# Keys and queries rounded on all rows and placed by transfers, tails in source order, the last joint by token tiles

## The chip, the cores and the metric

The kernel runs on one core of one Trainium2 chip. The metric is the device time of one execution in microseconds (us). PE is the tensor engine, DVE the vector engine, ACT the scalar engine, POOL GpSimd; SP is the engine that issues most DMA transfers, in the order of its program.

## The reference

Two layers of a diffusion backbone work on 256 latent and 256 context tokens of width 1024. Each layer is a half-step SwiGLU, a mixer (retention and differential attention side by side) and a second half-step SwiGLU, each between two RMS norms with shift, scale and gate from a conditioning vector. In the second layer only the latent tokens go on behind the mixer's keys and values.

```python
def modulate(x, g, shift, scale):
    return rmsnorm(x, g) * (1.0 + scale) + shift

def add_residual(x, y, g_post, gate, weight):
    return x + weight * gate * rmsnorm(y, g_post)

def swiglu(h, w_in, w_out):
    a, b = jnp.split(h @ w_in, 2, axis=-1)
    return (jax.nn.silu(a) * b) @ w_out

def diff_attend(q, k, v, lam):
    s = jnp.einsum('bhiqd,bhikd->bhiqk', q, k).astype(jnp.float32) * (DIFF_DH ** -0.5)
    p = jax.nn.softmax(s, axis=-1)
    a = p[:, :, 0] - lam * p[:, :, 1]
    return jnp.einsum('bhqk,bhke->bhqe', a.astype(v.dtype), v)
...
for l in range(DEPTH):
    x = add_residual(x, swiglu(modulate(x, ...)), nw[1], mod[:, 2], 0.5)
    y, yc = token_mixer(h, hc, ...)          # 8 heads of diff_attend, two maps of 64 each; 4 heads of retention
    x = add_residual(x, y, nw[3], mod[:, 5], 1.0)
    x = add_residual(x, swiglu(modulate(x, ...)), nw[5], mod[:, 8], 0.5)
```

Queries and keys of the latent tokens are rotated (rope_2d) before the scores.

## The kernel before, in words

The tokens are four tiles of 128 rows, X0 and X1 latent (LAT), X2 and X3 context (CTX). Every product is three matmuls (`mm3`, L330 to L332): a number is held as a rounded high part and a low part, and high x high, high x low and low x high are summed in PSUM. Weights come as slabs of 128 x 1024 through four raw buffers (`load`, SP's queue) and are split by ACT (L154) and DVE (L155) into one of five buffers; 24 matmuls of 512 columns use a slab. The order in which each engine runs its instructions is fixed before the program starts, by a list scheduler with costs of its own; where the code says `tc.manual_schedule` an engine keeps the order of the source.

A **tail** ends a feed-forward or a mixer: four tiles of 24 matmuls each (two halves of 12), then per tile `post_norm` (Square L317, product L319, residual L325) and, for the next stage, the norm of the two latent tiles: Square L267, mean and power on POOL (L254 to L257), `xn` L270 on DVE, 16 transposes on PE (L280), scale and shift on ACT (L289), high and low parts on DVE (L292, L293). The **last joint** is the place in layer 1 where the mixer ends and the last feed-forward begins; only two tiles are left there.

A mixer has four **blocks** of differential attention (0 to 3), two heads each. `projT` makes the block's transposed keys for all tokens (48 matmuls), then its queries; its result lies in a pair of PSUM banks (main4) until `ev_diff` has taken it out: rotation by quarters (L547, four L550, L552), then high and low parts in 64-row pieces (ACT L571, L575, L577, L578; DVE L572, L576). Each map's tile holds its own 64 rows beside a copy that meets the query's low part, so that a score is two matmuls, L660 with the keys' high and L661 with their low parts. For each head and token tile (a tile of the attention): two maps of scores in a PSUM pair of four banks (side4), row maximum (DVE L662), two exponentials (ACT L665), the difference of the maps (DVE L669, L671, L673), four transposes (PE L682), a copy (ACT L684), four matmuls with the values (L694), and behind the last tile a norm (L699 to L713). Layer 0 has eight such tiles a block, layer 1 four. Between these steps the scheduler puts projections of the next parts on PE.

Of the kernel before, what the change touches and what calls it, by code (L numbers as in the profile page):

```python
# [18 lines left out]
P = 128  # L19
D = 1024  # L20
# [14 lines left out]
def build(ctx, tc, a):  # L35
# [216 lines left out]
    def rstd_2(ss):  # L252
        m = small(2, "pm")
        pool.tensor_scalar(out=m[:, 0:1], in0=ss[:, 0:1], scalar1=1.0 / D, scalar2=EPS, op0=ALU.mult, op1=ALU.add)  # L254
        pool.tensor_scalar(out=m[:, 1:2], in0=ss[:, 1:2], scalar1=1.0 / D, scalar2=m[:, 0:1], op0=ALU.mult, op1=ALU.add)
        r = small(1, "pr")
        pool.tensor_tensor(out=r, in0=m[:, 1:2], in1=cneg[:, 0:1], op=ALU.pow)  # L257
        return r

    def norm_xn(c, alloc):  # L260
        xs = []
        for j in range(2):
            t = 2 * c + j
            ss = small(2, "ss")
            for hf in range(2):
                junk = jp.tile([P, 512], BF16, tag="ja", name="ja")
                act(junk, X[t][:, hf * 512:(hf + 1) * 512], AF.Square, accum_out=ss[:, hf:hf + 1])  # L267
            r = rstd_2(ss)
            xn = alloc([P, D])
            dve.tensor_scalar(out=xn, in0=X[t], scalar1=r, scalar2=None, op0=ALU.mult)  # L270
            xs.append(xn)
        return xs
# [33 lines left out]
    def start(AB):  # L306
        h = new_h()
        norm_pair(LAT, AB, h)
        return h, None

    def post_norm(t, yb, Gb, out=None):
        c = t // 2
        ss = small(2, "ss")
        us = []
        for hf in range(2):
            junk = jp.tile([P, 512], BF16, tag="ja", name="ja")
            act(junk, yb[hf], AF.Square, accum_out=ss[:, hf:hf + 1])  # L317
            u = tmp2()
            dve.tensor_tensor(out=u, in0=yb[hf], in1=Gb[c][:, hf * 512:(hf + 1) * 512], op=ALU.mult)  # L319
            us.append(u)  # L320
            banks.put(yb[hf])
        r = rstd_2(ss)
        for hf in range(2):
            xs = X[t][:, hf * 512:(hf + 1) * 512]
            dve.scalar_tensor_tensor(out=xs, in0=us[hf], scalar=r, in1=xs, op0=ALU.mult, op1=ALU.add)  # L325
            if out is not None:
                nc.sync.dma_start(out[t][:, hf * 512:(hf + 1) * 512], xs)

    def mm3(o, wH, wL, xH, xL, start, stop):
        mm(o, lhsT=wH, rhs=xH, start=start, stop=False)  # L330
        mm(o, lhsT=wH, rhs=xL, start=False, stop=False)  # L331
        mm(o, lhsT=wL, rhs=xH, start=False, stop=stop)  # L332

# [19 lines left out]
    def ffn(l, i, st, AB, fetch, pairs, side, nside, after=None, out=None):  # L353
# [17 lines left out]
        if begun is not None:  # L371
            f0 = len(begun)
            for f in range(f0):
                fin_ev(f, begun[f])
        elif len(pairs) == 2:
            w01 = [fin_w(l, i, 0), fin_w(l, i, 1)]
            ab01 = [[bank(), bank()], [bank(), bank()]]
            fin_mm((0, 1), w01, ab01, 0, 256)
            xs = norm_xn(CTX, tmp4)
            for q in range(4):  # L380
                norm_q(CTX, q, xs, AB, h)
            fin_mm((0, 1), w01, ab01, 256, 512)
            for f in range(2):
                fin_ev(f, ab01[f])
            f0 = 2
# [10 lines left out]
        for f in range(f0, NF):  # L396
            w = fin_w(l, i, f, pin=len(pairs) == 1 and f < 2)
# [39 lines left out]
        tail = [fout_w(NP - 2), fout_w(NP - 1)]  # L437
# [3 lines left out]
        for t in range(NT):  # L441
            for hf in range(2):
                for e in range(2):
                    for j in range(2):
                        fout_mm(t, j, tail[e][0], tail[e][1], False, e == 1 and j == 1, (hf,))
            post_norm(t, y[t], Gb, out)
            if t == 1 and after is not None:
                after()
        slots.put(*tail[0][1], *tail[1][1], *Gb.values())

    def mixer(l, st, AB, fetch, after):
# [69 lines left out]
        def projT(b, pairs, ev, w):  # L521
# [18 lines left out]
            for c in pairs:  # L540
                ev(c, bk[:, :, c * 256:(c + 1) * 256])
# [22 lines left out]
        def ev_diff(H, Lo):  # L564
            def ev(c, b):
                q = rotate(b, dtab, 32) if c == LAT else b
                sl = slice(c * 256, (c + 1) * 256)
                for m in range(2):
                    own, oth = slice(64 * m, 64 * m + 64), slice(64 - 64 * m, 128 - 64 * m)
                    if Lo is None:  # L570
                        act(H[m][own, :, sl], q[own], AF.Copy, scale=0.125)  # L571
                        dve.scalar_tensor_tensor(out=H[m][oth, :, sl], in0=q[own], scalar=0.125,  # L572
                                                 in1=H[m][own, :, sl], op0=ALU.mult, op1=ALU.subtract)
                    else:
                        nc.scalar.copy(H[m][own, :, sl], q[own])  # L575
                        dve.tensor_tensor(out=Lo[m][own, :, sl], in0=q[own], in1=H[m][own, :, sl], op=ALU.subtract)  # L576
                        nc.scalar.copy(H[m][oth, :, sl], q[own])  # L577
                        nc.scalar.copy(Lo[m][oth, :, sl], Lo[m][own, :, sl])  # L578
            return ev
# [291 lines left out]
        def diff_blocks(u, before=None):  # L871
            KH = [slot([P, 2, 512], F32R) for _ in range(2)]
            KL = [slot([P, 2, 512], F32R) for _ in range(2)]
            projT(8 + u, BOTH, ev_diff(KH, KL), 0.3)
# [3 lines left out]
            projT(4 + u, QP, ev_diff(Q, None), 0.3)  # L878
# [73 lines left out]

        NT = 2 * len(QP)
# [20 lines left out]
        fin_early(l, 1, ((0, 0), (0, 1), (1, 0))[:1 if NQ == 2 else 3])  # L974
        Gb = fetch()
        for t in range(NT):
            for hf in range(2):
                for k in range(2 * n0, 8):
                    wo_mm(t, k, w[k - 2 * n0], False, k == 7, (hf,))
            post_norm(t, yb[t], Gb)  # L980
            if t == 1:
                after()
        slots.put(*M.values(), *Gb.values())

# [102 lines left out]
    AB, st0 = startup()  # L1087
    box = [st0]
    for l in range(L):
# [5 lines left out]
        ffn(l, 0, box.pop(), AB, F0, (LAT, CTX), chain(g0, gs1, g1, gs2), 24,  # L1095
            after=lambda: box.append(start(AB1)))
        mixer(l, box.pop(), AB1, F1, after=lambda: box.append(start(AB2)))
        g2, F2 = ada_gate(l, 2, 0.5)
        if last:
            ffn(l, 1, box.pop(), AB2, F2, (LAT,), g2, 5, out=a["out"])  # L1100
        else:
            gs, AB = ada_shsc(l + 1, 0)
            ffn(l, 1, box.pop(), AB2, F2, (LAT, CTX), chain(g2, gs), 13, after=lambda: box.append(start(AB)))


def rope_tables():
# [10 lines left out]
    dt = np.stack([np.concatenate([c, c, c, c], 1), np.concatenate([-s, s, -s, s], 1)], 0)  # L1117
# [10 lines left out]
def layout(i):  # L1128
# [14 lines left out]
    cols[3072:5120] = cols[3072:5120].reshape(32, 2, 2, 16).transpose(0, 2, 1, 3).reshape(-1)  # L1143
# [27 lines left out]
```

## Time and profile before

| | us |
|---|---|
| median of three runs (lowest, highest) | 2194.53 (2194.24, 2195.38) |
| the profiled execution | 2194.1 |
| its span, first to last instruction | 2192.3 |
| PE busy | 2140.4 |
| DVE busy | 1365.7 |
| ACT busy | 865.8 |
| POOL busy | 129.1 |

The clock granted to PE was 0.996 in the mean. The profiled execution is one of the same speed as the runs, so its durations can be set against them. A duration printed for a matmul holds its latency; what the next one waits for is read from start to start. "Idle before" names the instruction whose end let an engine go on.

### The profile page before, as it was taken

The page shows a single profiled execution, that of the slowest core. Times are in us where ns is not written, and L with a number is a line of the kernel's source. Part 1 is how long each engine was busy: PE and PEld are TensorE (multiplying, and loading weights), DVE is VectorE, ACT ScalarE, POOL GpSimd, SP SyncE. Part 2 cuts the span into 40 slices and gives each one's busy share as a digit, 9 for nine tenths or more (in the row PEclk, how much of TensorE's full clock was granted, in tenths as well). Part 3 has the DMA queues.
Part 4 walks back from the last instruction along what each step waited for, and adds up shares of the span by engine and source line. Part 5 has one row for each costly group of instructions (what it writes and reads, how often), then busy time and mean ns, then how long its engine had stood idle before and what let it go on. Part 6 is the DMA issues. An engine that isn't in the chain of part 4 may idle for free. (4 is left out here: it accounts for less than half of the span.)

```text
span 2192.3 us, 27590 instructions
## 1 busy us (share of the span) xinstructions
PE 2140.4 (98%) x10730; PEld 1790.6 (82%) x10730; DVE 1365.7 (62%) x2108; ACT 865.8 (39%) x1367; POOL 129.1 (6%) x236
## 2 busy tenths in 40 slices
PE   7999999999999999999999999999999999998998
PEld 5888888778788878888888888888878888878997
DVE  4799372678665774596243279825347776787554
ACT  3322332553533553522232242223245544565453
POOL 1000000201010000200000010000010000001000
PEclk9999999999999999999999999999999999999999
DMA  8866342222122234364334247734323323355554
GB/s 332 284 218 217 106 135 96 88 68 85 51 91 98 68 97 148 132 211 155 97 124 139 91 161 224 269 96 134 97 67 109 115 93 108 123 194 174 187 183 134
DMA packets 85060, 306.99 MB, mean 140 GB/s; under 512 B 9968, under 2 KB 10048, under 8 KB 84928
## 3 DMA queue, kind: packets, MB, share of 16 engines
q1 hardware_dynamic: 81936, 296.78, 41.2%
q0 software_dynamic: 2848, 8.43, 1.4%
q8 instruction: 84, 1.38, 0.3%
q14 instruction: 48, 0.39, 0.1%
q10 hardware_dynamic: 144, 0.01, 0.0%
HBM read 304.10 MB, written 1.09 MB: 139 GB/s over the span
## 5 line engine op out<-in xcount | busy, mean ns | idle before, releaser
L155 DVE TENSOR_TENSOR w<-raw,w 128x1024 fp32r<-128x1024 f32 x408 | 497.2, 1222 | 465.6 <-ACT w L154 461.9
L154 ACT CAST w<-raw 128x1024 fp32r<-128x1024 f32 x408 | 427.5, 1053 | 665.4 <-PE ps L332 609.3
L330 PE MATMUL ps<-h,w 128*128 128x512 f32 (+1 forms) x1868 | 664.7, 357 | 4.7 <-ACT w L154 2.6
L331 PE MATMUL ps<-h,w 128*128 128x512 f32 (+1 forms) x1868 | 664.9, 356 | 0.4 <-DVE h L293 0.3
L332 PE MATMUL ps<-h,w 128*128 128x512 f32 (+1 forms) x1868 | 663.6, 356 | 1.2 <-DVE w L155 1.2
L330 PEld LDWEIGHTS ps<-h,w 128*128 128x128 f32 x1868 | 353.4, 190 | 57.2 <-DVE h L292 4.7
L332 PEld LDWEIGHTS ps<-h,w 128*128 128x128 f32 x1868 | 353.8, 190 | 50.6 <-DVE w L155 1.8
L331 PEld LDWEIGHTS ps<-h,w 128*128 128x128 f32 x1868 | 354.1, 190 | 50.2 <-DVE h L293 1.4
L174 DVE CUSTOM_DVE_ANT_0 jd<-r,r 128x1024 bf16<-128x1024 f32 x224 | 273.4, 1221 | 6.8 <-DMA r<-wada_dram 2.0
L330 PE MATMUL ps<-w,h 128*128 128x512 f32 x544 | 216.1, 398 | 15.5 <-ACT r L577 11.9
L331 PE MATMUL ps<-w,h 128*128 128x512 f32 x544 | 214.3, 394 | 0.0
L332 PE MATMUL ps<-w,h 128*128 128x512 f32 x544 | 213.8, 394 | 0.0
L330 PE MATMUL ps<-w,gs 128*128 128x512 f32 x504 | 196.2, 389 | 0.0
L331 PE MATMUL ps<-w,gs 128*128 128x512 f32 x504 | 196.1, 389 | 0.0
L332 PE MATMUL ps<-w,gs 128*128 128x512 f32 x504 | 196.1, 389 | 0.0
L366 ACT ACTIVATE t<-ps 128x512 f32<-128x512 f32 (+1 forms) x88 | 47.9, 545 | 252.0 <-PE ps L332 250.6
L330 PEld LDWEIGHTS ps<-w,h 128*128 128x128 f32 x544 | 102.7, 189 | 38.2 <-ACT r L577 15.2
L367 DVE TENSOR_TENSOR r<-ps,t 128x512 f32<-128x512 f32 (+1 forms) x88 | 54.8, 622 | 105.3 <-PE ps L332 77.7
L331 PEld LDWEIGHTS ps<-w,h 128*128 128x128 f32 x544 | 102.8, 189 | 20.2 <-DVE w L155 1.5
L332 PEld LDWEIGHTS ps<-w,h 128*128 128x128 f32 x544 | 102.5, 188 | 20.4
L330 PEld LDWEIGHTS ps<-w,gs 128*128 128x128 f32 x504 | 94.6, 188 | 19.8
L332 PEld LDWEIGHTS ps<-w,gs 128*128 128x128 f32 x504 | 94.6, 188 | 19.6
(180 smaller groups left out, 2132.8 us busy)
## 6 DMA issues: line engine op xcount, KB each, us to landing
raw<-fin_dram SPq DMA_DIRECT2D x176, 512.0 KB, 4.3
r<-wada_dram SPq DMA_DIRECT2D x144, 512.0 KB, 5.1
raw<-fout_dram SPq DMA_DIRECT2D x88, 512.0 KB, 3.6
raw<-winW_dram SPq DMA_DIRECT2D x80, 512.0 KB, 3.6
raw<-winT_dram SPq DMA_DIRECT2D x48, 512.0 KB, 3.6
raw<-wout_dram SPq DMA_DIRECT2D x16, 512.0 KB, 5.6
r<-scr POOLq DMA_DIRECT2D x10, 512.0 KB, 5.4
r<-cc_dram SPq DMA_DIRECT2D x7, 512.0 KB, 5.2
```

The source lines that it names most:

```text
L154: keep(nc.scalar.copy(w[:, 0, :], src))
L155: keep(dve.tensor_tensor(out=w[:, 1, :], in0=src, in1=w[:, 0, :], op=ALU.subtract))
L174: dve.tensor_tensor_reduce(out=junk, in0=r[j], in1=cs[c], scale=1.0, scalar=0.0, op0=ALU.mult, op1=ALU.add, accum_out=out[:, c, 2 * u + j: ...
L330: mm(o, lhsT=wH, rhs=xH, start=start, stop=False)
L331: mm(o, lhsT=wH, rhs=xL, start=False, stop=False)
L332: mm(o, lhsT=wL, rhs=xH, start=False, stop=stop)
L366: act(sg[:, :N], ab[0][:, :N], AF.Silu)
L367: dve.tensor_tensor(out=g[f // 2][:, f % 2, :N], in0=ab[1][:, :N], in1=sg[:, :N], op=ALU.mult)
```

## The change

Four edits. `norm_x` takes the norm's sum of squares in one Square of 1024 columns instead of two, with one POOL step less. `tail` runs PE in the order of the source: the latent norm's transposes stand between the two halves of the fourth tile. Keys and queries are rotated by halves of 64 rows and split for all 128 rows at once (`ev_full`, context first), and transfers on SP's queue (`move`) place the pieces of 32 rows in the maps' tiles: twelve for the keys and eight for the queries of a block, 160 in all; the weight columns and the rotation table are laid out to suit. `last_joint` replaces the last joint: output projection by token tiles, norm and transposes of each tile as it is done, and the first three pieces of the next feed-forward (`head`) with tokens stationary, tile by tile.

```diff
+    def norm_x(t, alloc):
+        ss = small(1, "sx")
+        junk = jp.tile([P, D], BF16, tag="ja", name="ja")
+        act(junk, X[t], AF.Square, scale=1.0 / 32, accum_out=ss)
+        m = small(1, "pm")
+        pool.tensor_scalar(out=m, in0=ss, scalar1=EPS, scalar2=None, op0=ALU.add)
+        r = small(1, "pr")
+        pool.tensor_tensor(out=r, in0=m, in1=cneg[:, 0:1], op=ALU.pow)
+        xn = alloc([P, D])
+        dve.tensor_scalar(out=xn, in0=X[t], scalar1=r, scalar2=None, op0=ALU.mult)
+        return xn
...
+    def tail(NT, part, finish, AB):
+        xs = []
+        with tc.manual_schedule(engines={nc.tensor.engine}):
+            for t in range(NT):
+                part(t, 0)
+                if t == 3 and AB is not None:
+                    h = new_h()
+                    for q in range(4):
+                        norm_q(LAT, q, xs, AB, h)
+                part(t, 1)
+                finish(t)
+                if t < 2 and AB is not None:
+                    xs.append(norm_x(t, tmp4))
+        return None if AB is None else (h, None)
...
+    def last_joint(l, M, fetch, AB):
...
+        with tc.manual_schedule(engines={nc.tensor.engine}):
             for hf in range(2):
...
+                part(0, range(8), hf)
+            post_norm(0, yb[0], Gb)
+            xs = [norm_x(0, tmp4)]
+            for hf in range(2):
+                part(1, range(4), hf)
...
+            part(1, range(4, 8), 0)
+            norm_tile(0, xs[0], AB, h)
+            part(1, range(4, 8), 1)
+            post_norm(1, yb[1], Gb)
+            xs.append(norm_x(1, tmp4))
+            fb = [bank() for _ in range(3)]
+            head(0)
+            norm_tile(1, xs[1], AB, h)
+            head(1)
...
-            for c in pairs:
+            for c in reversed(pairs):
                 ev(c, bk[:, :, c * 256:(c + 1) * 256])
...
+        def move(dst, md, src, ms, n):
+            for rd, rs in zip(rows_of(md), rows_of(ms)):
+                nc.sync.dma_start(dst[rd, :, 0:n].bitcast(F32), src[rs, :, 0:n].bitcast(F32))
+
+        def ev_full(H, Lo, scale):
             def ev(c, b):
-                q = rotate(b, dtab, 32) if c == LAT else b
+                q = rotate(b, dtab, 64) if c == LAT else b
                 sl = slice(c * 256, (c + 1) * 256)
...
+                act(H[:, :, sl], q, AF.Copy, scale=scale)
+                dve.scalar_tensor_tensor(out=Lo[:, :, sl], in0=q, scalar=scale, in1=H[:, :, sl],
+                                         op0=ALU.mult, op1=ALU.subtract)
             return ev
...
-            projT(8 + u, BOTH, ev_diff(KH, KL), 0.3)
+            projT(8 + u, BOTH, ev_full(KH[0], KL[0], 1.0), 0.5)
+            for K2 in (KH, KL):
+                move(K2[1], 1, K2[0], 1, 512)
+                move(K2[1], 0, K2[0], 1, 512)
+                move(K2[0], 1, K2[0], 0, 512)
             if before:
                 before()
             Q = [slot([P, 2, 512], F32R) for _ in range(2)]
-            projT(4 + u, QP, ev_diff(Q, None), 0.3)
+            qH, qL = tmp4([P, 2, 512], F32R), tmp4([P, 2, 512], F32R)
+            projT(4 + u, QP, ev_full(qH, qL, 0.125), 0.5)
+            for m in range(2):
+                move(Q[m], m, qH, m, 256 * NQ)
+                move(Q[m], 1 - m, qL, m, 256 * NQ)
             return KH, KL, Q
```

In the new code `mm3` is L340 to L342, a score L780 and L781, its row maximum L782, exponential L785, difference L789 to L793, transposes L802, copy L804, weighing L814; the eviction is L668 to L673 (rotation), L696 and L697, a move L690, the norm's `xn` L268, `norm_tile` L359 to L369.

The change also moves instructions that it doesn't name. On PE, in block 2 of layer 0, the attention's first tile has just been scored; before, twelve more matmuls of a projection (L330 to L332, weights from the right, tokens h) stand ahead of these rows:

```order
L330 MATMUL ps<-w,h 128x512
L331 MATMUL ps<-w,h 128x512
L332 MATMUL ps<-w,h 128x512
L660 MATMUL ps<-r_5273,r_5359 128x512
L682 MATMUL ps<-ident,t_5474 128x128 x4
L661 MATMUL ps<-r_5275,r_5359 128x512
L660 MATMUL ps<-r_5274,r_5360 128x512
L661 MATMUL ps<-r_5276,r_5360 128x512
L330 MATMUL ps<-w,h 128x512
L694 MATMUL ps<-r_5051,t_5517 128x128 x2
L694 MATMUL ps<-r_5052,t_5517 128x128 x2
L682 MATMUL ps<-ident,t_5505 128x128 x4
```

The same place on PE now, from the second map's scores of the first two tiles (L780, L781) to the transposes of the second (L802):

```order
L780 MATMUL ps<-r_5253,r_5337 128x512
L781 MATMUL ps<-r_5255,r_5337 128x512
L780 MATMUL ps<-r_5253,r_5337 128x512
L781 MATMUL ps<-r_5255,r_5337 128x512
L780 MATMUL ps<-r_5252,r_5336 128x512
L802 MATMUL ps<-ident,t_5455 128x128 x4
L781 MATMUL ps<-r_5254,r_5336 128x512
L780 MATMUL ps<-r_5253,r_5337 128x512
L781 MATMUL ps<-r_5255,r_5337 128x512
L814 MATMUL ps<-r_5030,t_5498 128x128 x2
L814 MATMUL ps<-r_5031,t_5498 128x128 x2
L802 MATMUL ps<-ident,t_5486 128x128 x4
```

The projection matmuls between the scores and the transposes are gone from here; they now stand ahead of the block's first score, 100 of them behind the query projection instead of 35.

On SP, the queue of the weight slabs, at the same block of the kernel before there are slabs alone (raw; winT for transposed projections, winW for wide ones):

```order
L147 DMA raw<-winW_dram 128x1024 x4
L147 DMA raw<-winT_dram 128x1024 x4
L147 DMA raw<-winW_dram 128x1024 x8
L147 DMA raw<-winT_dram 128x1024 x4
L147 DMA raw<-winW_dram 128x1024 x4
```

And now, with the keys' (r_5252 to r_5255) and the queries' moves (r_5336, r_5337):

```order
L147 DMA raw<-winT_dram 128x1024 x3
L690 DMA r_5253<-r_5252 32x1024 x4
L690 DMA r_5255<-r_5254 32x1024
L690 DMA r_5252<-r_5252 32x1024 x2
L690 DMA r_5255<-r_5254 32x1024 x3
L690 DMA r_5336<-t_5338 32x1024
L690 DMA r_5254<-r_5254 32x1024 x2
L690 DMA r_5336<-t_5338 32x1024
L690 DMA r_5336<-t_5339 32x1024 x2
L690 DMA r_5337<-t_5338 32x1024 x2
L690 DMA r_5337<-t_5339 32x1024 x2
L147 DMA raw<-winT_dram 128x1024
```

Twenty moves stand between two slabs, and the last of the keys' moves comes behind the first of the queries'.

## Rows read from the trace of the kernel before

**Rows 1.** The page, parts 1 and 2: PE, its clock, the transfer rate, 40 slices.

```profile
PE 2140.4 (98%) x10730; PEld 1790.6 (82%) x10730; DVE 1365.7 (62%) x2108; ACT 865.8 (39%) x1367; POOL 129.1 (6%) x236
...
PEclk9999999999999999999999999999999999999999
...
GB/s 332 284 218 217 106 135 96 88 68 85 51 91 98 68 97 148 132 211 155 97 124 139 91 161 224 269 96 134 97 67 109 115 93 108 123 194 174 187 183 134
```

**Rows 2.** The waits of PE: us in total, times, the longest.

```profile
PE ps L280 <- DVE t L270: 12.7, 10, 4.9
PE ps L330 <- ACT r L577: 11.9, 8, 1.7
...
PE ps L330 <- DVE t L550: 3.2, 1, 3.2
```

**Rows 3.** Timeline of PE, layer 0, block 0, behind the query projection.

```profile
448.70 0.50 PE L330 MATMUL ps<-w,h 128*128 128x512 f32 x1 [1.66 <-ACT r L577]
```

**Rows 4.** Timeline of ACT at the same place.

```profile
448.07 0.58 ACT L577 CAST r<-ps 64x512 fp32r<-64x512 f32 x1
```

**Rows 5.** Timeline of PE, layer 1, block 3.

```profile
1922.67 0.47 PE L330 MATMUL ps<-w,h 128*128 128x512 f32 x1 [3.21 <-DVE t L550]
...
1924.09 0.50 PE L330 MATMUL ps<-w,h 128*128 128x512 f32 x1 [0.95 <-ACT r L577]
...
1925.07 0.63 PE L330 MATMUL ps<-w,h 128*128 128x512 f32 x1
...
1929.46 0.39 PE L330 MATMUL ps<-w,h 128*128 128x512 f32 x1
...
1932.18 0.39 PE L660 MATMUL ps<-r,r 128*128 128x512 f32 x1
```

**Rows 6.** Timeline of PE in the first tail and in the third.

```profile
390.80 0.65 PE L280 MATMUL ps<-ident,t 128*128 128x128 f32 x4 [1.29 <-DVE t L270]
...
392.63 1.53 PE L280 MATMUL ps<-ident,t 128*128 128x128 f32 x12 [0.48 <-DVE t L270]
...
1262.36 2.75 PE L280 MATMUL ps<-ident,t 128*128 128x128 f32 x12 [0.48 <-DVE t L270]
```

**Rows 7.** Timeline of PE at the last joint.

```profile
1993.63 1.11 PE L280 MATMUL ps<-ident,t 128*128 128x128 f32 x4 [4.92 <-DVE t L270]
...
1995.47 2.82 PE L280 MATMUL ps<-ident,t 128*128 128x128 f32 x12 [0.72 <-DVE t L270]
```

**Rows 8.** DMA issues: count, KB each, median us to landing.

```profile
raw<-winT_dram SPq DMA_DIRECT2D x48, 512.0 KB, 3.6
...
out_dram<-X SPq DMA_DIRECT2D x4, 256.0 KB, 2.1
```

**Rows 9.** Timeline of DVE: blocks 2 and 3, layers 0 and 1.

```profile
718.63 1.22 DVE L662 TENSOR_REDUCE mx<-ps 128x2 f32<-128x1024 f32 x1
...
721.82 0.75 DVE L673 SCALAR_TENSOR_TENSOR t<-t,r 128x512 f32<-128x512 f32 x1
...
747.94 0.48 DVE L673 SCALAR_TENSOR_TENSOR t<-t,r 128x256 f32<-128x256 f32 x1
...
780.16 2.36 DVE L662 TENSOR_REDUCE mx<-ps 128x2 f32<-128x1024 f32 x2
...
812.98 0.48 DVE L673 SCALAR_TENSOR_TENSOR t<-t,r 128x256 f32<-128x256 f32 x1
...
1889.32 2.36 DVE L662 TENSOR_REDUCE mx<-ps 128x2 f32<-128x1024 f32 x2
...
1903.56 0.75 DVE L673 SCALAR_TENSOR_TENSOR t<-t,r 128x512 f32<-128x512 f32 x1
...
1929.66 1.23 DVE L662 TENSOR_REDUCE mx<-ps 128x2 f32<-128x1024 f32 x1 [0.49 <-PE ps L661]
...
1935.46 0.74 DVE L673 SCALAR_TENSOR_TENSOR t<-t,r 128x512 f32<-128x512 f32 x1
...
1947.82 0.75 DVE L673 SCALAR_TENSOR_TENSOR t<-t,r 128x512 f32<-128x512 f32 x1
```

More of the change, by code (lines that the diff above doesn't have):

```diff
@@ L315, in post_norm @@
         for hf in range(2):
-            junk = jp.tile([P, 512], BF16, tag="ja", name="ja")
-            act(junk, yb[hf], AF.Square, accum_out=ss[:, hf:hf + 1])
+            junk = jp.tile([P, D], BF16, tag="ja", name="ja")
+            act(junk[:, 0:512], yb[hf], AF.Square, scale=1.0 / 32, accum_out=ss[:, hf:hf + 1])
             u = tmp2()
@@ L332, in mm3, with split2, norm_tile @@
         mm(o, lhsT=wL, rhs=xH, start=False, stop=stop)
+    def split2(src):
+        w = [slot([P, 2, 512], F32R) for _ in range(2)]
+        wv = [z.rearrange("p a n -> p (a n)") for z in w]
+        nc.scalar.copy(wv[0], src)
+        dve.tensor_tensor(out=wv[1], in0=src, in1=wv[0], op=ALU.subtract)
+        return wv, w
+    def norm_tile(t, xn, AB, h):
+        A, B = AB
+        ts = slice(t * P, (t + 1) * P)
+        for q2 in range(2):
+            bk = bank()
+            b = bk.rearrange("p (k n) -> p k n", k=4)
+            for kk in range(4):
+                k = 4 * q2 + kk
+                nc.tensor.transpose(b[:, kk], xn[:, k * P:(k + 1) * P], ident)
+            hf = tmp2([P, 4, P])
+            for kk in range(4):
+                k = 4 * q2 + kk
+                act(hf[:, kk, :], b[:, kk], AF.Identity, bias=B[:, t // 2, k:k + 1], scale=A[:, t // 2, k:k + 1])
+            banks.put(bk)
+            for q in (2 * q2, 2 * q2 + 1):
+                hv = hf[:, 2 * (q % 2):2 * (q % 2) + 2]
+                hH = h[q][:, :, 0, ts]
+                dve.tensor_copy(hH, hv)
+                dve.tensor_tensor(out=h[q][:, :, 1, ts], in0=hv, in1=hH, op=ALU.subtract)
     early = {}
@@ L351, in fin_part, with ffn @@
                         h[k // 2][:, k % 2, 1, c0:c1], fresh and k == 0, k == KD - 1)
-    def ffn(l, i, st, AB, fetch, pairs, side, nside, after=None, out=None):
+    def ffn(l, i, st, AB, fetch, pairs, side, nside, nxt=None, out=None):
         h, begun = st
@@ L370, in ffn @@
         f0 = 0
-        if begun is not None:
+        if isinstance(begun, dict):
+            g.update(begun)
+            f0 = 3
+        elif begun is not None:
             f0 = len(begun)
@@ L396, in ffn @@
         for f in range(f0, NF):
-            w = fin_w(l, i, f, pin=len(pairs) == 1 and f < 2)
+            w = fin_w(l, i, f, pin=False)
             ab = [bank(), bank()]
@@ L436, in ffn @@
         cs.clear()
-        tail = [fout_w(NP - 2), fout_w(NP - 1)]
+        last2 = [fout_w(NP - 2), fout_w(NP - 1)]
         if i == 1 and l < L - 1:
@@ L440, in ffn, with part @@
         Gb = fetch()
-        for t in range(NT):
-            for hf in range(2):
[L443 to L451, printed above, removed]
+        def part(t, hf):
+            for e in range(2):
+                for j in range(2):
+                    fout_mm(t, j, last2[e][0], last2[e][1], False, e == 1 and j == 1, (hf,))
@@ L452, in mixer @@
+    def mixer(l, st, AB, fetch, nxt):
         h = st[0]
@@ L562, in ev_ret, with rows_of @@
             return ev
-        def ev_diff(H, Lo):
+        def rows_of(m):
+            return [slice(32 * m + 64 * x, 32 * m + 64 * x + 32) for x in range(2)]
+        def move(dst, md, src, ms, n):
+            for rd, rs in zip(rows_of(md), rows_of(ms)):
+                nc.sync.dma_start(dst[rd, :, 0:n].bitcast(F32), src[rs, :, 0:n].bitcast(F32))
+        def ev_full(H, Lo, scale):
             def ev(c, b):
-                q = rotate(b, dtab, 32) if c == LAT else b
+                q = rotate(b, dtab, 64) if c == LAT else b
                 sl = slice(c * 256, (c + 1) * 256)
[L568 to L578, printed above, removed]
+                act(H[:, :, sl], q, AF.Copy, scale=scale)
+                dve.scalar_tensor_tensor(out=Lo[:, :, sl], in0=q, scalar=scale, in1=H[:, :, sl],
+                                         op0=ALU.mult, op1=ALU.subtract)
             return ev
@@ L951, in mixer @@
         flush()
+        if last:
+            return last_joint(l, M, fetch, nxt)
         NT = 2 * len(QP)
@@ L973, in mixer, with part @@
         w = sum((wo_w(u) for u in range(n0, 4)), [])
-        fin_early(l, 1, ((0, 0), (0, 1), (1, 0))[:1 if NQ == 2 else 3])
+        fin_early(l, 1, ((0, 0),))
         Gb = fetch()
[L976 to L982, printed above, removed]
+        def part(t, hf):
+            for k in range(2 * n0, 8):
+                wo_mm(t, k, w[k - 2 * n0], False, k == 7, (hf,))
+        st = tail(NT, part, lambda t: post_norm(t, yb[t], Gb), nxt)
         slots.put(*M.values(), *Gb.values())
+        return st
     def startup():
@@ L1094, in build @@
         gs2, AB2 = ada_shsc(l, 2)
[L1095 to L1097 removed]
+        st = ffn(l, 0, st, AB, F0, (LAT, CTX), chain(g0, gs1, g1, gs2), 24, AB1)
+        st = mixer(l, st, AB1, F1, AB2)
         g2, F2 = ada_gate(l, 2, 0.5)
         if last:
[L1100 removed]
+            ffn(l, 1, st, AB2, F2, (LAT,), g2, 5, out=a["out"])
         else:
             gs, AB = ada_shsc(l + 1, 0)
[L1103 removed]
+            st = ffn(l, 1, st, AB2, F2, (LAT, CTX), chain(g2, gs), 13, AB)
 def rope_tables():
```

94 lines of the change are left out of this document (70 added, 24 removed).

## The prediction

> **What bounds the kernel now.** I read the page's parts 1 and 2 first: the tensor engine (PE) is busy 2140.4 of 2192.3 us and its clock stands at nine tenths or more in every slice of the page [rows 1]. So the time is the matmul work plus the gaps in it, and a change that leaves the products alone can only move gaps. The second view, the waits of PE, lists them: 12.7 us for the normalised rows that the transposes of L280 want, 11.9 us in eight waits for a cast of the key eviction (L577), 3.2 us for a rotation (L550) [rows 2]. The rest is the program's start and smaller waits, which the change doesn't touch. Third, the timelines at these places. At 448.70 PE has idled 1.66 us for a PSUM pair [rows 3] that the scalar engine (ACT) is still emptying with L577 at 448.07 [rows 4], the last but one of a dozen 64-row casts by which a key projection is evicted. In layer 1 the same place costs more: 3.21 and 0.95 us, and behind them the granted clock falls to the lower of its two levels, 1.2 GHz: eight matmuls at 0.43 us each (1925.07 is one) where twelve take 2.72 us, 0.2267 each, from 1929.46 to 1932.18 [rows 5]. The durations printed are latencies; these start-to-start pitches are what work costs: 0.227 us for 512 columns, half of it for 256 (an estimate), about 0.11 for a transpose (twelve in 1.53 us with the last one's latency [rows 6]).
>
> The profiled execution took 2194.1 us, 1.8 outside the span; the median of the runs shown is 2194.53. I sum against 2194.1. What a measurement of this kernel can tell from no change is about 0.2%, 4.4 us.
>
> **The tails.** Each of four tails stalls twice before L280, 1.29 and 0.48 us [rows 6], because the 16 transposes stand behind 64 of 96 matmuls, 16 of them after the last one of tile 1. The new order puts 36 there. What they must cover follows from the old stall: 16 x 0.227 + 1.29 = 4.9 us for the first transposes, and with 4 transposes, 3 matmuls and the second stall 6.5 us for tile 1; 36 x 0.227 = 8.2 us covers both. Gain 4 x 1.77 = 7.1. The single 1024-wide Square and the POOL step left out shorten a chain that is now hidden: nothing. If the cover failed, the 1.77 would come back a tail. At one tail (1262.36) the twelve transposes took 2.75 instead of 1.53 us, at the low clock after the idle time [rows 6]: 1.2 more. Tails: 8.3.
>
> **The last joint.** It idles 4.92 and 0.72 us, and its transposes run at the low clock (2.82 for twelve instead of 1.53; 1.11 for four instead of 0.65) [rows 7]: 7.4 us in sum. In the new order tile 0 is covered by 36 matmuls (8.2 us against 6.5), and tile 1 by head(0), 72 of 256 columns, 8.2 us. But head(1) wants all of tile 1's rows, and after its eight transposes nothing is left to cover ACT's and DVE's making of them: of these eight scale-and-shift steps and the first high and low parts I take 3 us as exposed (bounds 0, and the old 5.6). Six more transposes are 0.7. Gain 7.4 - 3.7 = 3.7.
>
> **The evictions.** K and Q are now rotated by halves (two L671 in place of four L550) and leave PSUM by one ACT and one DVE step of each token half, some seven steps of 0.6 to 0.7 us on two engines in place of twenty: about 4 to 5 us, the context half first. PE asks for the pair after Q's projection of 48 matmuls, 10.9 us (5.5 in layer 1). Seven of the eight L577 waits go: 11.9 - 0.95 = 10.9 us. The eighth, with the 3.21 us of L550 and the slow clock behind it [rows 5], is K of block 3 in layer 1, whose eviction stands behind block 2's softmax on DVE in both orders; I leave its cost as it is (bounds: it all goes, 5.7 us more gain, or it doubles).
>
> **The moves.** 160 transfers of at most 128 KB, 20 a block on SP's queue. The nearest rows are 2.1 us to landing for 256 KB and 3.6 for a weight slab of 512 KB [rows 8]. Q's eviction (5 us), eight moves of 1 MB in all (3.2 us at the 332 GB/s of the first slice [rows 1], an estimate) and one landing make 10 to 12 us behind Q's last matmul. In the new order 92 to 120 matmuls, 20.8 to 27 us, stand between Q's projection and the block's first score, so the moves are hidden. SP is in order: 20 moves wait for Q's eviction with the next weight slabs behind them, some 8 us late; the slabs loaded ahead (four raw and five split buffers, 24 matmuls or 5.4 us each) are worth more. Cost 0; without that cover, up to 3.6 us for each slab that is late. The Trainium skill, "DMA: Bandwidth & Descriptors", section "Rules for kernel authors", says that two transfers to disjoint partition halves serialize and advises one wide transfer; with its fit of 2.0 us plus bytes at 436 GB/s an estimate is 20 x 2.3 = 46 us a block. That speaks against placing keys in 32-row pieces; no run here shows such a transfer yet.
>
> **Where the attention moved.** This is the loss. Before, the first score of a block stood 35 matmuls behind Q's projection; now 92 to 120. The projections that used to stand between the softmax steps are spent before them. In blocks 0 and 1 of each layer 4.98 us of matmuls still stand between the last score of the first tile and its transposes. A tile's softmax, from the row maximum (718.63) to the end of L673 (721.82 + 0.75), took 3.94 us [rows 9]: covered. In blocks 2 and 3 it is not: there the order leaves 0.68, 1.80, 1.74 and 1.81 us, and PE, in order, must wait. Lower bound, the first tile alone: 3.3 + 2.1 + 2.2 + 2.1 = 9.7 us. Upper bound: the whole chain of the block, from the first row maximum to the end of the last L673, keeps its length, 29.8, 33.3, 15.0 and 18.9 us [rows 9]; the matmul work of the order in that stretch falls from 26.7 to 19.0, 30.0 to 23.9, 13.7 to 9.2 and 17.3 to 11.0. (For the first: 44 projection matmuls instead of 76, 10 wide scores instead of 12, 16 narrow ones, 44 transposes and weighings: 10.0 + 2.3 + 1.8 + 4.8 = 18.9.) Less what the old order lost there anyway (3.1, 3.3, 1.3, 1.6): 7.7 + 6.1 + 4.5 + 6.3 = 24.6 us. I take 18, nearer the top: tiles 3 and 4 can't score before the first two have emptied their PSUM pairs, and in block 2 of layer 0 not one projection matmul stands between the first four tiles. Behind block 3 of layer 1 the gate transposes and the output projection wait too: 1.5 (0 to 4).
>
> **Sum.** -8.3 - 3.7 - 10.9 + 18 + 1.5 = -3.4 us: 2190.7, on the runs' median 2191.
>
> **The rivals.**
> *The dense attention costs only its first tiles.* For it: a key eviction takes ten casts from ACT and four steps from DVE, so the later tiles may find both free. Against it: the PSUM pairs. 9.7 instead of 18: 2182, and with block 3's eviction of layer 1 off the path 2177.
> *The softmax queues behind weight splitting (slower).* In block 3 of layer 1 the first tile took 6.54 us (1929.66 to the end of its L673 at 1936.20) with two L155 and two gate steps ahead of it on DVE. In the old order 6.6 us of matmuls hid that; in the dense blocks no more than 1.8 us do. 6.5 us for the first tile of the four is 20 us, and 2.6 more for each later pair (3 + 3 + 1 + 1) is 21: 41 instead of 18, 2214. It decides from 21.4 us in the four blocks, 5.4 a block: above that the kernel is not faster.
> *The moves come later than their cover.* If the pieces of a block went one behind the other, 20 x 2.1 = 42 us, of which K's twelve start 11 us before Q's end, some 10 to 15 us a block would show, 80 to 120 in all: 2290. Against it: the first slice moves 332 GB/s [rows 1] while 512 KB land in 3.6 us [rows 8], which is over two transfers under way at once. The Trainium skill's rule on serializing would be this case.
> *Nothing comes of the eviction.* Then 10.9 us are not gained and it ends near 2202; only with an eviction of over 10.9 us, which its steps don't add up to.
>
> **How the numbers follow.** Forecast with its neighbours (2185 to 2198) 0.42, first rival 0.22, second 0.27, moves 0.04, no gain 0.05. The range leaves out the moves, the far end of the second rival and the very best case: from all bounds at their best, -8.3 - 7 - 16.6 + 9.7 = -22 (2172), to dense blocks at 24.6 and 4 behind them, with no gain at the joint, +9.4, and a part of the queueing on top: 2208. The forecast's own range is 2185 to 2198. Faster by over 0.2% (below 2190.1): half of the forecast's 0.42 and the first rival, 0.44; slower (above 2198.9): second rival, moves, and no gain, 0.34; the rest 0.22.
>
> **What would show it.** In the waits of PE after the change: no L696 or L697 (the new eviction) with more than a us or two, except in block 3 of layer 1; L280 gone from the four tails; at the last joint one wait of about 3 us at L359 or L340. New lines must appear: L802 waiting for L793, L780 for L785, in blocks 2 and 3 only, 10 to 25 us together. If L780 waits for a DMA, the moves are late. The forecast is wrong if the new waits sum to less than 12 or more than 25 us, or if they stand in blocks 0 and 1 as well.

## The result and the profile after

The changed kernel took 2213.31 us (2212.27 to 2213.59, four executions), the kernel before 2194.39 beside it: ratio 1.0085, 95% interval 1.0068 to 1.0103. (Every ratio here is to the kernel before, measured beside the kernel that is named.) It is slower by 19 us; 2191 was forecast, in a range up to 2208.

The page of the changed kernel, parts 1 and 2, answers to [rows 1]:

```profile
PE 2150.4 (97%) x10736; PEld 1805.5 (82%) x10736; DVE 1317.6 (60%) x2059; ACT 802.0 (36%) x1239; POOL 111.1 (5%) x194
...
PEclk9999999999999999999999999999999999899999
```

DVE and ACT have 48 and 64 us less to do and POOL 18: the work went away as meant. PE has nearly the same matmuls (10736 for 10730), so its gaps have grown. Its waits, us in total, times, the longest:

```profile
PE ps L340 <- DVE t L671: 6.0, 2, 3.0
PE ps L341 <- DVE w L155: 4.3, 3, 2.9
PE ps L981 <- ACT t L804: 3.8, 1, 3.8
PE ps L780 <- ACT t L785: 3.8, 2, 3.0
PE ps L342 <- DVE w L155: 3.4, 2, 2.9
PE ps L814 <- ACT t L804: 3.3, 6, 0.7
```

L280's 12.7 us and the eight waits for the eviction's casts [rows 2] are gone, and no score waits for a transfer. What came instead lies inside the attention blocks: scores waiting for exponentials (L785), weighings for copies (L804), projections for a rotation (L671) or for a weight slab that stands behind softmax steps on DVE (L155).

To sum this up by place I took from the trace the time from each matmul's start to the next one's, less the pitch of the earlier one, which is that time in an undisturbed stretch (0.2266 us for 512 columns, 0.1195 for 256, 0.110 for a transpose or weighing). The rest, the gap, holds idle time and slow-clock matmuls alike. In us, with two of the experiments below (e9 and e12):

| place | before | after | e9 | e12 |
|---|---|---|---|---|
| four tails | 14.7 | 6.2 | 6.2 | 6.2 |
| layer 0, blocks 0 and 1 | 4.8 | 17.8 | 2.8 | 5.8 |
| layer 0, blocks 2 and 3 | 5.6 | 15.7 | 4.3 | 15.5 |
| layer 1, blocks 0 and 1 | 1.5 | 1.9 | 1.9 | 2.5 |
| layer 1, blocks 2 and 3 | 2.7 | 26.1 | 2.2 | 22.4 |
| between the blocks (evictions) | 23.7 | 6.8 | 6.3 | 3.1 |
| last joint and just ahead of it | 9.4 | 4.7 | 4.1 | 4.1 |
| all else (start, end) | 18.8 | 20.9 | 20.9 | 20.7 |
| sum | 81.1 | 100.1 | 48.7 | 80.4 |

Tails, evictions and joint give 30 us; the blocks take 47. The end of block 0 of layer 0, on PE in the changed kernel:

```profile
503.48 0.39 PE L342 MATMUL ps<-h,w 128*128 128x512 f32 x1
504.66 0.41 PE L802 MATMUL ps<-ident,t 128*128 128x128 f32 x2 [0.79 <-DVE es L819]
505.53 0.71 PE L814 MATMUL ps<-r,t 128*128 128x128 f32 x4 [0.46 <-ACT t L804]
...
506.97 0.71 PE L814 MATMUL ps<-r,t 128*128 128x128 f32 x4 [0.52 <-ACT t L804]
510.66 0.80 PE L340 MATMUL ps<-w,h 128*128 128x512 f32 x1 [2.98 <-DVE t L671]
511.25 0.63 PE L341 MATMUL ps<-w,h 128*128 128x512 f32 x1
```

Behind 503.48 no projection is left, and the softmax of the last tiles shows as waits of transposes (L802) and weighings (L814). Then the next projection waits 2.98 us for PSUM, and behind the idle time its matmuls run at the lower clock level (granted 0.50 from 511.25 to 515.50; ten matmuls at 0.427 us). DVE in the same block, its idle time in brackets:

```profile
476.83 2.35 DVE L782 TENSOR_REDUCE mx<-ps 128x2 f32<-128x1024 f32 x2 [6.40 <-PE ps L781]
...
484.74 0.68 DVE L681 SCALAR_TENSOR_TENSOR r<-ps,r 128x512 fp32r<-128x512 f32 x1
...
507.59 0.68 DVE L668 TENSOR_TENSOR t<-ps,rtab 128x512 f32<-128x512 f32 x1
...
509.92 0.69 DVE L671 TENSOR_TENSOR t<-ps,rtab 64x512 f32<-64x512 f32 x1
```

Two things stand in these rows. The first score ran at 469.83, yet the first row maximum comes 7.0 us later: it needs both maps, and the order has the second map's first score at 476.18, 28 matmuls behind the first map's. In the kernel before the two are 1.5 us apart, on PE and on DVE:

```profile
457.01 0.50 PE L660 MATMUL ps<-r,r 128*128 128x512 f32 x1
```

```profile
458.50 2.35 DVE L662 TENSOR_REDUCE mx<-ps 128x2 f32<-128x1024 f32 x2
```

And the retention's keys, whose context half leaves PSUM at 484.74 (L681), wait until 507.59 for the rotation of their latent half (L668), behind the whole attention. PE's wait at 510.66 is for that PSUM: the last step that reads it there (L671) ends at 510.61. In layer 1 the queue is another. DVE and PE, block 2:

```profile
1908.35 2.35 DVE L782 TENSOR_REDUCE mx<-ps 128x2 f32<-128x1024 f32 x2 [1.50 <-PE ps L781]
1910.62 1.21 DVE L155 TENSOR_TENSOR w<-raw,w 128x1024 fp32r<-128x1024 f32 x1
```

```profile
1911.89 0.55 PE L342 MATMUL ps<-h,w 128*128 128x256 f32 x1 [2.89 <-DVE w L155]
```

A weight slab's low part, for which ACT was done at 1907.06, stands behind two row maxima that themselves waited for scores. Later in that block the granted clock falls. Two windows: bounds, length, busy time of PE, PEld (weight loads), DVE, ACT and POOL with their instructions, then PE's granted clock, the DMA share and GB/s:

```profile
1906.00:1929.00 23.00, 17.51 (x105) 15.62 (x104) 16.83 (x25) 13.68 (x27) 0.00 (x0) 0.85 0.49 164
1929.00:1937.00 8.00, 6.00 (x19) 4.65 (x18) 5.95 (x14) 1.10 (x3) 1.02 (x1) 0.57 0.00 0
```

### The profile page after: what moved, and what is told of

It is laid out like the page before. It is cut to its first block, busy times and chain, and to the rows that moved or that the text cites. A ratio compares the mean times of both kernels' runs of the same rounds, so it can differ in the third digit from the quotient of the medians.

```text
span 2211.8 us, 27624 instructions
## 1 busy us (share of the span) xinstructions
PE 2150.4 (97%) x10736; PEld 1805.5 (82%) x10736; DVE 1317.6 (60%) x2059; ACT 802.0 (36%) x1239; POOL 111.1 (5%) x194
## 5 line engine op out<-in xcount | busy, mean ns | idle before, releaser
L155 DVE TENSOR_TENSOR w<-raw,w 128x1024 fp32r<-128x1024 f32 x399 | 486.1, 1221 | 458.1 <-ACT w L154 455.0
L340 PE MATMUL ps<-h,w 128*128 128x512 f32 (+1 forms) x1820 | 653.4, 360 | 6.0 <-ACT w L154 3.0
L342 PE MATMUL ps<-h,w 128*128 128x512 f32 (+1 forms) x1820 | 652.1, 359 | 3.5 <-DVE w L155 3.4
L154 ACT CAST w<-raw 128x1024 fp32r<-128x1024 f32 x399 | 418.9, 1055 | 650.2 <-PE ps L342 578.5
L341 PE MATMUL ps<-h,w 128*128 128x512 f32 (+1 forms) x1820 | 652.0, 359 | 0.4 <-DVE h L293 0.3
L340 PEld LDWEIGHTS ps<-h,w 128*128 128x128 f32 x1820 | 345.2, 190 | 58.5 <-DVE h L292 4.7
L342 PEld LDWEIGHTS ps<-h,w 128*128 128x128 f32 x1820 | 345.4, 190 | 53.1 <-DVE w L155 4.4
L341 PEld LDWEIGHTS ps<-h,w 128*128 128x128 f32 x1820 | 345.6, 190 | 50.3 <-DVE h L293 1.4
L340 PE MATMUL ps<-w,h 128*128 128x512 f32 (+1 forms) x552 | 218.8, 398 | 9.4 <-DVE t L671 6.0
L341 PE MATMUL ps<-w,h 128*128 128x512 f32 (+1 forms) x552 | 218.5, 396 | 4.4 <-DVE w L155 4.3
L342 PE MATMUL ps<-w,h 128*128 128x512 f32 (+1 forms) x552 | 217.3, 394 | 0.0
L340 PE MATMUL ps<-w,gs 128*128 128x512 f32 x504 | 196.2, 389 | 0.0
L342 PE MATMUL ps<-w,gs 128*128 128x512 f32 x504 | 196.1, 389 | 0.0
L340 PEld LDWEIGHTS ps<-w,h 128*128 128x128 f32 x552 | 105.8, 192 | 31.8 <-DVE t L671 6.7
L341 PEld LDWEIGHTS ps<-w,h 128*128 128x128 f32 x552 | 105.6, 191 | 26.9 <-DVE w L155 7.0
L342 PEld LDWEIGHTS ps<-w,h 128*128 128x128 f32 x552 | 105.6, 191 | 21.5 <-DVE h L293 0.4
L342 PEld LDWEIGHTS ps<-w,gs 128*128 128x128 f32 x504 | 94.6, 188 | 19.8
L340 PEld LDWEIGHTS ps<-w,gs 128*128 128x128 f32 x504 | 94.6, 188 | 19.7
```

Of the source, the lines that this page charges most:

```text
L154: keep(nc.scalar.copy(w[:, 0, :], src))
L155: keep(dve.tensor_tensor(out=w[:, 1, :], in0=src, in1=w[:, 0, :], op=ALU.subtract))
```

## The experiments

**Which part loses.** e1 is the change without the placement of K and Q, e2 that placement alone in the kernel before; e7 adds to e1 one line of the placement:

```diff
-            for c in pairs:
+            for c in reversed(pairs):
                 ev(c, bk[:, :, c * 256:(c + 1) * 256])
```

> Everything of the change but the placement of keys and queries: they are evicted in 64-row pieces as before. The comparison of the two traces puts the gain of the four tails at 8.6 us and of the last joint at 7.3, and the loss in the attention blocks. Theory (the loss is the attention moved behind its cover): 2194.4 - 8.6 - 7.3 = 2178, with a range of 2175 to 2182. Rival (tails and joint themselves disturb the mixers that follow them, and the gains seen in the trace are only shifted): 2188 or more.

> The kernel before with only the new eviction and the transfers of keys and queries. Theory: the blocks lose 47 us and the waits for the key eviction give back 14, so 2194.4 + 33 = 2227 (2220 to 2232). Rival (the loss comes from the parts together, for instance from tails that end at another point of the weight stream): near 2200.

> e1_tails_joint (2182.6: all of the change but the placing of K and Q) with one line of the placement kept: K's projection evicts its context half first. It moves no row, and the first scores stand 48 matmuls behind Q's last. Theory (the eviction's waits of the kernel before come from ScalarE's first cast waiting for VectorE's rotation, which a half without rotation spares; 11.9 us of waits): 2171 us (2168 to 2180). Rival (the four casts and six other steps of the old eviction still queue, and the later scores take the rest): 2182 us or more.

Measured: e1 2182.58 (ratio 0.9942, 0.9928 to 0.9957), e2 2217.91 (1.0103, 1.0088 to 1.0118), e7 2173.32 (0.9907, 0.9892 to 0.9922). So the placement is the part that loses, 23 us, and the rest gains 13; together they lose 9 more than their sum. The waits of PE for the eviction, in e1 and in e7:

```profile
PE ps L340 <- ACT r L698: 11.9, 8, 1.7
...
PE ps L340 <- DVE t L671: 3.2, 1, 3.2
```

```profile
PE ps L340 <- DVE t L671: 5.3, 8, 1.0
```

The context half first takes 10 us of these waits away (15.1 to 5.3) without moving a row, and some 8 us of the time (by the ratios).

e8 is the changed kernel with the old last joint: the call of `last_joint` is taken out, and the old code with its own early weight loads stands there again.

> The changed kernel with the old last joint (the old order and loads there, all else of the change kept). If the three parts add up, it gives back what the joint earned, 8.55 - 1.25 = 7.3 us: 2220 us (2217 to 2223). If the joint's early loads and weight splits collide with the softmax of the last attention block, which the placement made late (the whole is 8 us worse than the sum of e1 and e2), the old joint takes nothing or gains: 2205 to 2211 us.

Measured: 2211.71 (1.0082, 1.0067 to 1.0097), against 2213.31: the parts don't add up. The gaps say why: at its place the new joint saves 7.1 us (8.4 to 1.25), but block 3 ahead of it grows from 7.2 to 12.2 and the stretch between them from 0.2 to 3.5. In the changed kernel ACT, and behind it PE, hold this there:

```profile
1975.09 1.04 ACT L347 CAST r<-raw 128x1024 fp32r<-128x1024 f32 x1 [2.30 <-DMA raw<-wout_dram]
1976.04 0.58 ACT L804 COPY t<-ps 128x512 f32<-128x512 f32 x1
```

```profile
1976.68 1.03 PE L981 MATMUL ps<-ident,t 128*128 128x128 f32 x4 [3.76 <-ACT t L804]
```

The joint's slab (L347) came late, the attention's copy stood behind it, and PE waited 3.76 us for that copy. In e1, where block 3 is not late, the joint keeps its gain.

**Transfers, or the later place?** e3 leaves all transfers out (the second map reads the first map's keys, and the queries are evicted straight into the tiles that the scores read). e4 is e3 with the transfers made to tiles that nothing reads. e5, e6 and e11 are e3 with the attention held back (the last number is 5 in e5, 8 in e6, 10 in e11):

```diff
-            if sideq:
+            if sideq and clock[0] >= sideq[0][4]:
...
-            defer(f"d{u}", diff_attn(u, *kq, dv), within, 4 * NQ + LAG + 1)
+            defer(f"d{u}", diff_attn(u, *kq, dv), within, 4 * NQ + LAG + 1, 8)
```

> The changed kernel without its 160 transfers: both maps' scores read the one tile that the eviction wrote, so the attention's numbers are other ones; operations and shapes of PE, DVE and ACT are the same. Its order has the first score 26 matmuls behind the query projection instead of 92 to 120. Theory: the blocks' loss goes and the evictions' gain stays, 2213 - 47 = 2166 (2162 to 2178). Rival (the one-piece eviction or the order of DVE behind it is the cause): 2200 or more.

> As the run without transfers, but 160 transfers of the same sizes on the same queue go to tiles that nothing reads, so that no score waits for them; the attention's numbers are other ones here too. Theory (only the wait and the place of the scores cost): within 4 us of the run without transfers. Rival (traffic, or SP standing still with weight slabs behind it): over 10 us slower than that run.

> The kernel of e3_no_transfers (no transfer at all; both maps read one tile, so the attention's numbers differ) with each attention held back at the moment it is handed to the matmul order: its first score stands 60 matmuls behind Q's last in every block, against 26 there. Theory (the changed kernel loses by the later place of the attention, not by a wait for a transfer): between e3's 2161.5 and e6_hold8, 2175 to 2190 us. Rival (a later place is harmless as long as nothing waits for a transfer): 2160 to 2168 us.

> As e5_hold5, held back further: first score 96 matmuls behind Q's last, where the changed kernel has it in most blocks, and still without a transfer (attention's numbers differ as in e3). Theory (the later place is the loss): near the changed kernel's 2213 less the 5.6 us that idle transfers cost in e4, so 2200 us (2192 to 2210), with the waits for L819's and L804's tiles at the ends of layer 0's blocks back. Rival (the transfers' landing or their traffic is the loss): 2160 to 2170 us.

> As e6_hold8 (no transfers; attention's numbers differ as in e3), held to 144 matmuls behind Q's last in the first three blocks, 33 us, which is past the changed kernel's first row maximum (30 us). Theory (there is a latest place, between 24 and 30 us behind Q for the first row maximum, past which the cover runs out): gaps of 6 us or more at the ends of layer 0's blocks and 2185 to 2215 us. Rival (lateness never matters here; what costs is that the two maps' scores stand apart, or the transfers): 2172 us or less.

Measured:

| kernel | first score behind Q, matmuls | us | ratio (95%) |
|---|---|---|---|
| e3 | 26 | 2161.50 | 0.9849 (0.9834 to 0.9864) |
| e4 | 26 | 2167.11 | 0.9877 (0.9861 to 0.9894) |
| e5 | 60 | 2159.87 | 0.9846 (0.9831 to 0.9860) |
| e6 | 96 | 2166.42 | 0.9876 (0.9859 to 0.9892) |
| e11 | 144 (first three blocks) | 2171.20 | 0.9886 (0.9871 to 0.9900) |

Moves that nothing reads cost 5.6 us, between the theory's 4 and the rival's 10. One place of layer 1 has a gap of 7.1 in e4, where e3 has under 2: PE waits 1.68 and 2.14 us for the two halves of a weight slab, and the slow clock follows. Whether the transfers' bytes make that, or their place in SP's queue and in the order, isn't shown.

My first theory, that a later first score by itself makes the loss, falls: at 96 matmuls e6 takes 47 us less than the changed kernel (5.6 of them for the moves, by e4), and e11, which the theory put at 2185 or more, loses no more than 10 against e3. What differs is in their rows. In e6 both maps' scores stand together, so the first row maximum comes 23.7 us behind Q's last matmul (29.9 in the changed kernel) and the last weighing starts at 497.27, while projections still run between the weighings. On DVE and PE:

```profile
470.19 2.35 DVE L782 TENSOR_REDUCE mx<-ps 128x2 f32<-128x1024 f32 x2
```

```profile
497.27 0.69 PE L814 MATMUL ps<-r,t 128*128 128x128 f32 x4
```

In e11 the attention ends at 511.8, later than in the changed kernel, but its code comes later too, and DVE has the retention's rotation ahead of the first row maximum:

```profile
480.77 0.68 DVE L668 TENSOR_TENSOR t<-ps,rtab 128x512 f32<-128x512 f32 x1
481.46 1.39 DVE L671 TENSOR_TENSOR t<-ps,rtab 64x512 f32<-64x512 f32 x2
482.88 1.23 DVE L782 TENSOR_REDUCE mx<-ps 128x2 f32<-128x1024 f32 x1
```

**The same transfers, another order.** e9 changes one line, and e13 is its control, with all moves on GpSimd's queue:

```diff
-            for rd, rs in zip(rows_of(md), rows_of(ms)):
-                nc.sync.dma_start(dst[rd, :, 0:n].bitcast(F32), src[rs, :, 0:n].bitcast(F32))
+            for i, (rd, rs) in enumerate(zip(rows_of(md), rows_of(ms))):
+                (nc.sync, pool)[i].dma_start(dst[rd, :, 0:n].bitcast(F32), src[rs, :, 0:n].bitcast(F32))
```

> The changed kernel with one line changed: of each pair of 32-row moves the second is issued from GpSimd's queue instead of SyncE's. The same transfers, but in the kernel's written-out order the first map's scores now stand 50 matmuls behind Q's last (96 before) and the second map's 15 behind those (28 before). First theory (a later first score alone is the loss) has fallen with e6_hold8. Theory now: the loss is that the second map's first score stands 124 matmuls behind Q, so that the first row maximum, which needs both maps, comes 30 us behind Q and the chain of softmaxes outlasts the projection that covers it; with 65 matmuls (15 us) the blocks' gaps return to some 2.5 us and the time to 2167 to 2180 us. Rival (attention that truly waits for its transfers loses by the transfers themselves, their landing or their traffic): 2195 us or more, with waits for a DMA at the first scores.

> The changed kernel with all its moves issued from GpSimd's queue instead of SyncE's, a control for e9_two_queues, which changed both the queue and the place of the scores. The first scores stay 99 matmuls behind Q and the second map's 28 behind those. Theory (the place in the order is the loss): 2195 to 2216 us. Rival (what helped in e9 was SyncE's queue, rid of the moves ahead of the weight loads): 2175 us or less.

e9: 2162.37 (0.9851, 0.9836 to 0.9865), 51 us less than the changed kernel, and 11 less than e7. The first scores of its two maps and the row maximum in block 0:

```profile
457.93 0.39 PE L780 MATMUL ps<-r,r 128*128 128x512 f32 x1
...
461.33 0.39 PE L780 MATMUL ps<-r,r 128*128 128x512 f32 x1
```

```profile
461.98 2.35 DVE L782 TENSOR_REDUCE mx<-ps 128x2 f32<-128x1024 f32 x2 [2.99 <-PE ps L781]
```

The row maximum comes 15.6 us behind Q's last matmul (446.37) and no score waits for a transfer. Yet a move of the keys takes longer to land than in the changed kernel (second fence):

```profile
r<-r SPq DMA_DIRECT2D x48, 128.0 KB, 4.0
r<-r POOLq DMA_DIRECT2D x48, 128.0 KB, 4.0
```

```profile
r<-r SPq DMA_DIRECT2D x96, 128.0 KB, 2.3
```

A block's last move lands only 1.7 us earlier behind Q (12.6 for 14.2 us in block 0). What changed more is the order fixed before the run: it puts the scores 50 and 65 matmuls behind Q instead of 100 and 128. e13: 2204.69 (1.0051, 1.0034 to 1.0068), with the scores at 99 and 127: the other queue brings 9 us, though one score now waits 1.1 us for a move; the other 42 come with the order. In e13 the gaps of layer 0's first two blocks are 6 to 7 us, block 0's chain from the first row maximum to the last weighing being 3.3 us shorter, and those of layer 1's last two some 30, as bad as ever.

e10 keeps SyncE's moves and lets PE run the blocks as the code writes them, the attention held to 60 matmuls (`tc.manual_schedule` around the blocks).

> The changed kernel, its transfers untouched, with TensorE's order through the four blocks as the code writes it, and the attention held to 60 matmuls (13.6 us) behind Q's last, both maps' scores together. Theory (the order is the loss, the transfers are not): the transfers land 14.7 us behind Q, so about 1 us of wait a block, and 2167 to 2185 us; the written order may add waits of its own, since it does not look at how long a softmax takes. Rival (the transfers are the loss): 2200 us or more.

2293.49 (1.0440, 1.0422 to 1.0457): the worst of all, and past the 2200 that was written for the rival. Its waits don't bear the rival out, but the run is no test of the theory either, since the written order brings waits of its own everywhere:

```profile
PE ps L340 <- DVE t L900: 27.1, 20, 5.2
...
PE ps L780 <- DMA r<-t: 5.1, 3, 1.8
```

The second line is of use: with the scores 60 matmuls behind Q, three do wait for a query move, 1.8 us at most. That bounds the true place of the transfers.

**The tie behind the attention.** e12 is the changed kernel with the rotation's scratch from another ring:

```diff
-            q, w = tmp2([P, 2, 256]), tmp2([P, 2, 256])
+            z = slot([P, 2, 512])
+            q, w = (z[:, i].rearrange("p (j n) -> p j n", j=2) for i in range(2))
+            slots.put(z)
```

> The changed kernel, with the two scratch tiles of a rotation taken from the ring of 20 slots instead of the ring of five t2 tiles, which the attention's transposed weights share. Transfers, queues and the places of the first scores stay (100 and 128 matmuls behind Q); but the rotation of the retention's K now stands on VectorE behind the third row maximum instead of behind the whole attention, so that PSUM comes free earlier and 111 matmuls of projection stand inside block 0 instead of 92. Theory (the late attention costs because the next projection's rotation, and with it the PSUM that the matmuls behind it need, is tied behind it): the gaps of layer 0's first two blocks fall from 8.9 to 4 us or less, 2195 to 2206 us in all. Rival (the tie is not what costs): 2210 us or more.

2193.20 (ten executions; 0.9995, 0.9985 to 1.0004): 20 us come back. The first scores stay 100 and 128 matmuls behind Q, the first row maximum 7.0 us behind the first score, and still the gaps of layer 0's first two blocks fall from 17.8 to 5.8; that is 12 of the 20, and layer 1's last two blocks and the evictions give 3.7 each. The attention itself isn't sooner done: its last weighing ends 63 us behind Q, in the changed kernel 61. On DVE the rotation (L670, L673 there) now runs at 484.70 instead of 507.59:

```profile
484.11 0.68 DVE L683 SCALAR_TENSOR_TENSOR r<-ps,r 128x512 fp32r<-128x512 f32 x1
484.70 0.68 DVE L670 TENSOR_TENSOR r<-ps,rtab 128x512 f32<-128x512 f32 x1
485.40 0.69 DVE L673 TENSOR_TENSOR r<-ps,rtab 64x512 f32<-64x512 f32 x1
```

so PSUM is free earlier, 111 projection matmuls stand inside the block instead of 92, and its last transposes wait for nothing but a short rest of softmax:

```profile
508.05 0.44 PE L804 MATMUL ps<-ident,t 128*128 128x128 f32 x2 [0.18 <-DVE t L795]
```

## Why the prediction was wrong

**The failed step** is "Where the attention moved", the sentence that blocks 0 and 1 are covered. It looked at the cover of the first tile, 4.98 us against 3.94, and booked nothing for the rest of the block. In layer 0 these two blocks cost 13.0 us, and the sign that the prediction had named for being wrong, waits in blocks 0 and 1 as well, is there. The cover, the projections that run on PE meanwhile, has an end: 192 matmuls behind Q, the last at 503.48, 56.5 us behind it. What stands after them needs the PSUM of the retention's keys, and the rotation that frees it shares five scratch tiles with the attention's transposed weights, which are handed out in the order of the code. The code writes the attention right behind Q; with its two maps' first scores 22.9 and 29.2 us behind Q, it ends at 61 us and holds the rotation until then. e12 shows the tie: there the attention ends at 63 us, and the gaps are back near those of the kernel before all the same (5.8 against 4.8). In e9 and e6 it ends at 45 and 51 us, before the cover does, and the tie costs nothing.

**The same step, blocks 2 and 3.** It forecast 18 us (9.7 to 24.6); measured 33.5. Layer 0's pair cost 10.1, inside its bounds of 5.4 and 13.8. Layer 1's pair cost 23.4 where the bounds were 4.3 and 10.8. The bounds took softmax chains against matmul work; they left out the slabs queued behind row maxima (2.89 us twice), the joint's early loads (5.0 us of block 3 by e8) and the slow clock behind each idle time. That layer 1's gaps vanish with the earlier scores is shown (2.2 in e9); how they divide between slabs, chain and clock isn't, and e12 and e13 leave them nearly whole.

Together the two make the miss: 13.4 us in blocks 0 and 1 of both layers and 15.5 more than forecast in blocks 2 and 3, against 8.7 of larger gains elsewhere (evictions 6.0, joint 2.5, tails 0.2); 2.1 came at the start and the end.

**The second rival** gave 2214, and the result is 2213, but by other terms, so the nearness is luck. Its 41 us lay all in the four blocks 2 and 3, where 33.5 came; 13.0 came where it had none, and the gains were larger than booked. Its mechanism, softmax and weight splitting in one DVE queue, stands in layer 1's rows, mostly the other way about: the split waits for the row maxima.

**Tails:** forecast -8.3, measured -8.5; the step held. **Last joint:** forecast -3.7 and +1.5 behind block 3. The joint's own gap fell by 7.3, so head(1) is covered better than the 3 us I exposed; with 2.6 lost just ahead of it, 4.7 is left. **Evictions:** forecast -10.9, measured -16.9; I left block 3 of layer 1 as it was, and there the 3.21 us and the slow clock behind them [rows 5] went as well. e7 shows that more than half of this gain, 10 us, is the order of the halves alone.

**The moves** were hidden, as forecast, and nearer to 14 than to the 10 to 12 us I worked out. SP's queue in block 0 of the changed kernel, Q's last matmul at 446.94:

```profile
455.07 4.39 SPq L690 DMA_DIRECT2D r<-t  x7
459.51 0.58 SPq L147 DMA_DIRECT2D raw<-winT_dram  x1
```

The last issue begins at 458.87 and ends at 459.46; a move lands 2.3 us behind the beginning of its issue, so the last one lands 14.2 us behind Q. The seven moves were issued in 4.39 us and landed 2.3 us each behind their issue, so their landings overlap.

The Trainium skill, "DMA: Bandwidth & Descriptors", section "Rules for kernel authors", has two transfers to disjoint partition halves serialize because both use the same DMA engines. Whole landings one behind the other, the 46 us a block estimated by that page, did not come; whether the bytes of these 32-row pieces go one behind the other this trace does not show, with an issue every 0.6 us. The fit behind that estimate is given on the page for transfers issued from GpSimd, and these were issued from SP.

What I did not see is that a hidden transfer can still cost. The scores were placed 8.7 us (first map) and 15.0 us (second map) behind the last landing. I had that order before me, with the two maps' scores apart, and counted only matmuls ahead of the first score. And the cost that I put at 0 was 5.6 us in e4, where nothing reads the moves.

## What to carry to other kernels

A transfer that lands in time can still cost through the order that was fixed around it: compare where its reader stands with where it lands, for each operand of the first step that needs all of them. When a stretch moves later, check its cover at the end as well as at the start, and ask which buffers it holds on to that the work behind it needs, scratch rings handed out in code order above all. Gains at one joint and losses at the next don't add up when they share a queue: e1 and e2 sum to +10 us and the whole was +19.

## What the runs showed of the hardware

Moves of 32 rows and 128 KB within SBUF landed 2.3 us behind the beginning of their issue on SP's queue, one issue every 0.6 us (changed kernel), and those of the keys 4.0 us when they were issued from SP and GpSimd in turn (e9). Twenty of them a block, read by nothing, cost 5.6 us (e4 against e3). In the changed kernel a wait of 3 us on PE was followed by about 4 us at 0.427 us a matmul instead of 0.227 (granted clock 0.50), so the idle time at the end of a block cost some 2 us more than it lasted.
